# An fp32 encoder trunk on one core: order of work at the start, on the way into each MLP and at its end

## The chip, the core and the metric

The kernel runs on one core of one Trainium2 chip. The metric is the device time of one execution in microseconds (us), of which several runs are taken; beside them one execution is profiled. The engines are named as in the profile: PE (TensorE, matmuls; PEld its weight loads), DVE (VectorE), ACT (ScalarE), POOL (GpSimd) and SP (SyncE, which here only issues transfers). Each engine works through its own queue in order.

## The reference

A trunk of two layers over 256 tokens of width 2048, all in fp32. Layer 0 mixes tokens by 2-D neighbourhood attention, layer 1 by grouped-query attention with rotary positions; in both, four more heads attend to 256 memory tokens. Each layer ends with a squared-ReLU MLP of width 8192:

```python
m = rms_norm(mem, mem_norm)
h = x
for i in range(DEPTH):
    n = rms_norm(h, attn_norm[i])
    ...            # projection, attention heads -> mix
    km, vm = jnp.split(m @ w_mem_kv[i], 2, axis=-1)
    cross = memory_attention(qm, km, vm)
    h = h + jnp.concatenate([mix, cross], axis=-1) @ w_o[i]
    n = rms_norm(h, mlp_norm[i])
    h = h + jnp.square(jax.nn.relu(n @ w_up[i])) @ w_down[i]
return rms_norm(h, final_norm)
```

## The kernel before, in words

**Products.** Each fp32 operand is split into a high part (ACT, a copy to fp32r, line 299) and a low part (DVE, the difference, line 300), and a product is three matmuls: high by high, high by low, low by high. Weights come from HBM as chunks of 128 x 2048 (1 MB). A chunk is split and used in two halves, and one half is a *grain*: the unit in which the program is written. `run_all` walks over the grains; `ahead(n)` writes the loads, additions and splits of grains up to 8, 5 and 4 places further on before grain n is written (`SOON`), and `tick` releases work that `later(n, ...)` put off by n grains. What is written is not the final order: a planner builds each engine's queue from dependencies, priorities and a timing model of its own, and may pull forward whatever is ready. `keep_in_program_order` (`pin`) and `issue_after` are the ways to hold it.

**Buffers.** Raw up chunks have two buffers (tag `U`), their halves `uh` and `ul` two each, first parts of down chunks two (`b`), the tag `T` two (scaled activations `h_s`, then the down steps' `t`, then `raw_T`). PSUM has eight banks: four for attention and transposes (`ps_att`), four for accumulators (`ps_acc`); between MLP part 1 and the last part they are replaced by eight named sums (`ps_sums`: `up`, `p1` to `p7`).

**Start.** The memory's transposed features (`memT`) and the first two chunks of `w_km` come in quarters; `begin` splits and multiplies them quarter by quarter. The memory's squares (`mem_squares`), their sums (`mem_stats`) and the scaling of the first keys (`km_done`, `put`) are put off by ticks, so that other work goes first. `add_mem` asks for four key chunks, then four value chunks.

**Way into the MLP.** The output projection is done in four blocks of 512 columns (`o_done(layer, nb)`). After three blocks a provisional scale per token is known (`guard`); block b of `h` is then scaled on ACT (`scaled`, line 610), transposed on PE (line 317) and split into `hT` (lines 324, 325). The exact factor (`inv`) is applied at the end of the MLP. The fourth block is added to `h` (line 630), scaled, transposed and split in the same way, and `hT` is complete.

**MLP.** The hidden width is cut into 8 parts of 8 chunks. Part 0's up products (`up_grains`, lines 670 to 672) come alone; the first half of a chunk needs `hT` 0 to 7, the second 8 to 15. Then each step has one up chunk of the next part beside one down step (`down_grains`) of the part before. A down step forms products of 2 x 2 blocks with seven instead of eight multiplications: its preparation `pre` adds two blocks (line 758, DVE) and lets POOL add two others by an accumulating transfer (line 759), `prep_first` splits `b` into `bh`, `bl`, and `prep_second` adds twice more (lines 767, 768) and splits `t` into `th`, `tl`. The last part is done in the classical way (`plain_grains`): per block of 512 columns two chunks, the first split in halves (`uh`, `ul`), the second in one piece of 2048 (`th`, `tl`, one buffer). In the last block of layer 1 the products of the first 128 tokens are all issued before those of the others, and `finish` scales and stores.

Of the kernel before, what the change touches and what calls it, by code (L numbers as in the profile page):

```python
# [17 lines left out]
P = 128  # L18
# [52 lines left out]
def encoder_kernel(ctx: ExitStack, tc: tile.TileContext, t: dict, out: bass.AP):  # L71
# [23 lines left out]
    def open_sums():  # L95
        at.att = opened("ps_att", space=bass.MemoryType.PSUM, bufs=4)
        at.acc = opened("ps_acc", space=bass.MemoryType.PSUM, bufs=4)
# [31 lines left out]
    nc.scalar.activation(warm, mhalf[:, :1], AF.Exp)  # L129

# [166 lines left out]
    def split(dst_hi, dst_lo, src):  # L297

        nc.scalar.activation(dst_hi, src, AF.Copy)  # L299
        nc.vector.tensor_tensor(dst_lo, src, dst_hi.bitcast(F32), op=ALU.subtract)  # L300
# [10 lines left out]
    def transposed(dst, src, ks, which):  # L311

        for a in range(0, len(ks), 2):
# [4 lines left out]
            for b, k in enumerate(ks[a : a + 2]):  # L318
                split_pair(dst, pt[:, b, :], which, k)

    def split_pair(dst, src, which, k):

        g = gain(which, k)
        nc.scalar.activation(dst[:, k, :SEQ], src, AF.Copy, scale=g)
        nc.vector.scalar_tensor_tensor(dst[:, k, SEQ:], src, g, dst[:, k, :SEQ].bitcast(F32),  # L325
                                       op0=ALU.mult, op1=ALU.subtract)
# [115 lines left out]
    def km_done(layer, hd):  # L442
        def f(w):
            if layer == 0:
                later((5, 5, 1, 1)[hd], put, w)
# [35 lines left out]
    def add_mem(layer):  # L481
        for hd in range(NMH):
            add_s(t[f"w_km{layer}"][hd], get("memT"), km_done(layer, hd))
        add_m([t[f"w_vm{layer}"][c] for c in range(4)], parts_of("memT"), vm_done(layer))

# [110 lines left out]

    def o_done(layer, nb):
        which = 2 * layer

        def guard():  # L600
# [4 lines left out]
            box["hT"] = wide(f"hT{layer}")  # L605

# [17 lines left out]
        def f(w):  # L624
# [3 lines left out]
            for i in range(NT):  # L628
                hs = h[:, i, nb * 512 : (nb + 1) * 512]
                nc.vector.tensor_tensor(hs, w.ps[i], hs, op=ALU.add)  # L630
                if nb < 3:
                    sum_squares(which, i, nb)
            if nb == GUARD - 1:
                later(1, guard)
                for b in range(GUARD):
                    later(2 + 2 * b, scaled, b)
            if nb == 3:
                later(1, scaled, 3)
                for i in range(NT):
                    sum_squares(which, i, nb)  # L640
                later(2, inv)
# [32 lines left out]
    def half_of_side(raw, hf):  # L674
        tiles = tuple(at.side.tile([P, HALF], F32R, tag=n, bufs=2, name=n) for n in ("uh", "ul"))
        split(*tiles, raw[:, hf * HALF : (hf + 1) * HALF])
# [7 lines left out]
    def up_grains(layer, part, m):  # L684
# [8 lines left out]
        def run(hf):  # L693
            if hf == 0:
                if part == 0:
                    own["ps"] = at.acc.tile([P, 512], F32, tag="acc", name="ps_u")[:, :SEQ]
                else:
                    if part == 1 and m == 0:
                        closed("ps_acc", "ps_att")
# [40 lines left out]
    def down_grains(layer, part, n, begins, ends):  # L740
# [10 lines left out]

        def block(k):
# [42 lines left out]
        return [Grain(lambda: run("first", FIRST), lambda: after(FIRST), load, pre, prep_first, SOON),  # L795
# [403 lines left out]
```

## Time and profile before

| | |
|---|---|
| median of 3 runs | 2070.88 us (2068.25 to 2073.3) |
| the profiled execution's own time | 2069.22 us |
| its span, first to last instruction | 2067.2 us |
| mean granted clock of PE | 0.997 |
| busy: PE, DVE, ACT, POOL | 2039.7, 1668.6, 1251.3, 119.2 us |
| matmuls | 12516 |
| read from HBM | 398.17 MB |

Durations come from one profiled execution. A row of the timeline gives start, duration, engine, line, operation, output and inputs, and in brackets the idle time of the engine before it and what ended that. Matmul ends are modelled: one record of 256 columns lasts 0.28 us, while the next starts about 0.11 later, so how many matmuls a stretch holds tells more than how long PE was busy in it. The clock granted to PE is 1.00 or about 0.5.

### The profile page before, as it was taken

To read this page: it belongs to the slowest core of one execution; us is meant where nothing else is said; L and a number is where in the kernel's file an instruction comes from. 1 tells how busy PE (TensorE), PEld (TensorE's weight loads), DVE (VectorE), ACT (ScalarE), POOL (GpSimd) and SP (SyncE) were. 2 spreads that over 40 slices of the span, in tenths; PEclk is the share of its full clock that TensorE was granted. 3 is DMA by queue.
4 is the path that set the end of the run, shared out by engine and by line. 5 is a ranking of instruction groups with operands and counts; after the bars stand their busy time and mean duration, and the time that the engine had idled before them with its cause. 6 is when DMAs were issued, how large, how long until landed. Compare 5 with 4: busy or idle time off the path is not lost.

```text
span 2067.2 us, 31544 instructions
## 1 busy us (share of the span) xinstructions
PE 2039.7 (99%) x12516; PEld 1815.0 (88%) x12516; DVE 1668.6 (81%) x2047; ACT 1251.3 (61%) x1642; POOL 119.2 (6%) x144
## 2 busy tenths in 40 slices
PE   8999999999999999999999999999999999999998
PEld 6888888889999999999988888889999999999996
DVE  6767667566899999999996667666988999999896
ACT  6755555555666666666656557555666666666653
POOL 0000000000010000010000001000000000000000
PEclk9999999999999999999999999999999999999999
DMA  7755555736777787787765454536877787777773
GB/s 266 297 183 177 189 175 170 274 105 202 223 235 231 218 240 225 225 240 226 231 201 209 171 177 143 188 138 197 232 227 227 224 242 222 233 232 223 232 225 121
DMA packets 92996, 433.78 MB, mean 210 GB/s; under 512 B 10416, under 2 KB 12080, under 8 KB 59568
## 3 DMA queue, kind: packets, MB, share of 16 engines
q1 hardware_dynamic: 75456, 399.25, 57.3%
q0 software_dynamic: 16816, 31.46, 8.6%
q8 instruction: 98, 1.61, 0.3%
q10 hardware_dynamic: 576, 1.05, 0.1%
q14 instruction: 50, 0.41, 0.1%
HBM read 398.17 MB, written 4.19 MB: 195 GB/s over the span
## 4 chain that ended last, share of the span: by engine, by line
PE 97%; DVE 1%; issue 1%; DMA 1%; ACT 0%; SPq 0%; POOLq 0%; POOL 0%; DVEq 0%; ACTq 0%
PE ps_u L672 11%; PE ps_u L670 11%; PE ps_u L671 11%; PE p L779 9%; PE p L780 9%; PE p L781 9%; PE ps_m L205 8%; PE ps_m L208 8%; PE ps_m L209 8%; PE ps_s L218 7%; PE ps_s L221 3%; PE pt_a L379 1%; PE pt_n L317 0%; PE av L387 0%; PE sc_ps L353 0%
## 5 line engine op out<-in xcount | busy, mean ns | idle before, releaser
L671 PE MATMUL ps_u<-hT,uh 128*128 128x256 f32 x2048 | 569.3, 278 | 3.7 <-DVE hT L325 3.6
L670 PE MATMUL ps_u<-hT,uh 128*128 128x256 f32 x2048 | 569.9, 278 | 1.5 <-ACT uh L299 1.5
L672 PE MATMUL ps_u<-hT,ul 128*128 128x256 f32 x2048 | 569.3, 278 | 1.5 <-DVE ul L300 1.3
L299 ACT ACTIVATE uh<-raw_U 128x1024 fp32r<-128x1024 f32 x278 | 295.0, 1062 | 325.2 <-PE ps_u L671 301.9
L300 DVE TENSOR_TENSOR lo<-raw,hi 128x1024 fp32r<-128x1024 f32 (+1 forms) x222 | 266.3, 1204 | 167.7 <-ACT hi L299 166.4
L671 PEld LDWEIGHTS ps_u<-hT,uh 128*128 128x128 f32 x2048 | 385.9, 188 | 9.1 <-DVE hT L325 4.5
L670 PEld LDWEIGHTS ps_u<-hT,uh 128*128 128x128 f32 x2048 | 386.3, 189 | 7.6 <-ACT uh L299 1.9
L672 PEld LDWEIGHTS ps_u<-hT,ul 128*128 128x128 f32 x2048 | 387.1, 189 | 3.0 <-DVE ul L300 2.3
L300 DVE TENSOR_TENSOR ul<-raw_U,uh 128x1024 fp32r<-128x1024 f32 x278 | 337.9, 1219 | 35.4 <-ACT uh L299 35.4
L299 ACT ACTIVATE hi<-raw 128x1024 fp32r<-128x1024 f32 (+1 forms) x222 | 231.3, 1047 | 218.7 <-PE ps_m L209 116.1
L299 ACT ACTIVATE th<-t 128x2048 fp32r<-128x2048 f32 x112 | 215.2, 1921 | 124.9 <-PE p L781 118.2
L300 DVE TENSOR_TENSOR tl<-t,th 128x2048 fp32r<-128x2048 f32 x112 | 256.3, 2288 | 40.3 <-ACT th L299 39.9
L300 DVE TENSOR_TENSOR bl<-b,bh 128x1536 fp32r<-128x1536 f32 x112 | 196.1, 1751 | 0.4
L780 PE MATMUL p<-tl,a_s 128*128 128x512 f32 x448 | 177.2, 396 | 0.0
L781 PE MATMUL p<-th,a_s 128*128 128x512 f32 x448 | 174.4, 389 | 0.0
L299 ACT ACTIVATE bh<-b 128x1536 fp32r<-128x1536 f32 x112 | 166.2, 1484 | 6.4
L779 PE MATMUL p<-th,a_s 128*128 128x512 f32 x448 | 166.1, 395 | 0.0
L759 POOL DMA_DIRECT2D t<-b x112 | 97.0, 866 | 1168.3 <-DVE t L758 377.5
L218 PE MATMUL ps_s<-nT,hi 128*128 128x512 f32 x448 | 141.7, 394 | 0.0
L781 PE MATMUL p<-bh,a_s 128*128 128x512 f32 x336 | 131.1, 390 | 0.0
L780 PE MATMUL p<-bl,a_s 128*128 128x512 f32 x336 | 130.9, 390 | 0.0
L758 DVE TENSOR_TENSOR t<-t,b 128x512 f32<-128x512 f32 x112 | 77.2, 690 | 48.2 <-DMA t<-in_w_pair 36.4
(235 smaller groups left out, 3510.6 us busy)
## 6 DMA issues: line engine op xcount, KB each, us to landing
raw_U<-in_w_up SPq DMA_DIRECT2D x128, 1024.0 KB, 6.6
b<-in_w_pair SPq DMA_DIRECT2D x112, 768.0 KB, 4.5
raw<-in_w_o SPq DMA_DIRECT2D x32, 1024.0 KB, 5.0
t<-in_w_pair SPq DMA_DIRECT2D x112, 256.0 KB, 3.4
t<-b POOLq DMA_DIRECT2D x112, 256.0 KB, 6.6
raw<-in_w_b SPq DMA_DIRECT2D x21, 1024.0 KB, 5.0
raw<-in_w_av SPq DMA_DIRECT2D x12, 1024.0 KB, 4.9
raw<-in_w_aq SPq DMA_DIRECT2D x12, 1024.0 KB, 4.9
```

The lines of the kernel that those rows point to most:

```text
L205: first = nc.tensor.matmul(w.ps[i], ah, hi[:, s], start=st, stop=False)
L208: nc.tensor.matmul(w.ps[i], ah, lo[:, s], start=False, stop=False)
L209: nc.tensor.matmul(w.ps[i], al, hi[:, s], start=False, stop=sp)
L218: nc.tensor.matmul(ps, hi[:, s], acts[:, k0 + j, :], start=k0 + j == 0, stop=False)
L299: nc.scalar.activation(dst_hi, src, AF.Copy)
L300: nc.vector.tensor_tensor(dst_lo, src, dst_hi.bitcast(F32), op=ALU.subtract)
L670: nc.tensor.matmul(ps, hi[:, s], acts[:, k, :SEQ], start=k == 0, stop=False)
L671: nc.tensor.matmul(ps, hi[:, s], acts[:, k, SEQ:], start=False, stop=False)
L672: nc.tensor.matmul(ps, lo[:, s], acts[:, k, :SEQ], start=False, stop=k == KT - 1)
L779: nc.tensor.matmul(ps, a[:, 0, ai, :], hi[:, s], start=begins, stop=False)
L780: nc.tensor.matmul(ps, a[:, 0, ai, :], lo[:, s], start=False, stop=False)
L781: nc.tensor.matmul(ps, a[:, 1, ai, :], hi[:, s], start=False, stop=ends)
```

## The change

Seven things are done at once.

- The accumulator banks are opened before the attention banks, so that the two groups change places, also against the eight named sums of the MLP.
- Eleven matmuls of ones by ones are issued at the start, into a tile that nobody reads.
- The memory's squares and their sums are put off by one tick more and the first two keys' `put` by two more; the value chunks are asked for between the second and the third key chunk.
- In `o_done` the fourth block is no longer added and then scaled: `begun` scales the old `h` early, two scalar_tensor_tensor add the scaled sum from PSUM, and the transposes follow at once. The residual add, the squares and `inv` come 4, 6 and 8 grains later, behind the last of `hT` on ACT and DVE (`past`).
- Additions and splits of the first two down steps are queued on ACT and DVE behind the up split that was fourth from last when they are written (`behind`).
- Part 0's up chunks go two by two: both first halves, then both second halves.
- In the classical part the second chunk is split in halves too, into separate tiles (`bh`, `bl` and `th`, `tl`), and has two grains.

```diff
@@ -93,8 +93,8 @@
         pass
 
     def open_sums():
+        at.acc = opened("ps_acc", space=bass.MemoryType.PSUM, bufs=4)
         at.att = opened("ps_att", space=bass.MemoryType.PSUM, bufs=4)
-        at.acc = opened("ps_acc", space=bass.MemoryType.PSUM, bufs=4)
 
     def open_ring():
         at.ring = opened("ring")
@@ -128,6 +128,10 @@
     warm = const.tile([P, 1], F32, name="warm")
     nc.scalar.activation(warm, mhalf[:, :1], AF.Exp)
 
+    idle = at.att.tile([P, P], F32, tag="att", name="idle")
+    for _ in range(11):
+        nc.tensor.matmul(idle, ones, ones, start=True, stop=True)
+
     def gain(which, k):
         return gains[:, which * KT + k : which * KT + k + 1]
 
@@ -296,8 +300,8 @@
 
     def split(dst_hi, dst_lo, src):
 
-        nc.scalar.activation(dst_hi, src, AF.Copy)
-        nc.vector.tensor_tensor(dst_lo, src, dst_hi.bitcast(F32), op=ALU.subtract)
+        first = nc.scalar.activation(dst_hi, src, AF.Copy)
+        return first, nc.vector.tensor_tensor(dst_lo, src, dst_hi.bitcast(F32), op=ALU.subtract)
 
     def rstd_of(ss, n, name):
 
@@ -316,13 +320,14 @@
                 for i in range(NT):
                     nc.tensor.transpose(pt[:, b, i * P : (i + 1) * P], src(i, k), ident)
             for b, k in enumerate(ks[a : a + 2]):
-                split_pair(dst, pt[:, b, :], which, k)
+                last = split_pair(dst, pt[:, b, :], which, k)
+        return last
 
     def split_pair(dst, src, which, k):
 
         g = gain(which, k)
-        nc.scalar.activation(dst[:, k, :SEQ], src, AF.Copy, scale=g)
-        nc.vector.scalar_tensor_tensor(dst[:, k, SEQ:], src, g, dst[:, k, :SEQ].bitcast(F32),
+        first = nc.scalar.activation(dst[:, k, :SEQ], src, AF.Copy, scale=g)
+        return first, nc.vector.scalar_tensor_tensor(dst[:, k, SEQ:], src, g, dst[:, k, :SEQ].bitcast(F32),
                                        op0=ALU.mult, op1=ALU.subtract)
 
     def along_free(r, res):
@@ -442,7 +447,7 @@
     def km_done(layer, hd):
         def f(w):
             if layer == 0:
-                later((5, 5, 1, 1)[hd], put, w)
+                later((7, 7, 1, 1)[hd], put, w)
             else:
                 put(w)
 
@@ -479,9 +484,13 @@
             nc.gpsimd.dma_start(box["vm"][:, :, i, :], mem_v[:, i])
 
     def add_mem(layer):
-        for hd in range(NMH):
-            add_s(t[f"w_km{layer}"][hd], get("memT"), km_done(layer, hd))
+        def add_km(hds):
+            for hd in hds:
+                add_s(t[f"w_km{layer}"][hd], get("memT"), km_done(layer, hd))
+
+        add_km((0, 1))
         add_m([t[f"w_vm{layer}"][c] for c in range(4)], parts_of("memT"), vm_done(layer))
+        add_km((2, 3))
 
     mem_sq = at.work.tile([P, 512], F32, tag="b_o", bufs=3, name="mem_sq")
 
@@ -594,6 +603,12 @@
         nc.vector.tensor_scalar(v, s, 1.0 / (n * 512), EPS, op0=ALU.mult, op1=ALU.add)
         return v
 
+    def past(fn, ins=None):
+
+        a, v = ins or box["ready"]
+        with tc.issue_after(a.ins), tc.issue_after(v.ins):
+            fn()
+
     def o_done(layer, nb):
         which = 2 * layer
 
@@ -603,6 +618,13 @@
             box["scale"] = keep.tile([P, NT], F32, tag="scale", name="scale")
             nc.gpsimd.tensor_tensor(box["scale"], box["near"], mhalf[:, :NT], op=ALU.pow)
             box["hT"] = wide(f"hT{layer}")
+
+        def begun():
+
+            y = at.side.tile([P, NT, 512], F32, tag="T", bufs=2, name="h_s")
+            for i in range(NT):
+                nc.scalar.activation(y[:, i, :], h[:, i, D - 512 :], AF.Copy, scale=box["scale"][:, i : i + 1])
+            box["begun"] = y
 
         def scaled(b):
             y = at.side.tile([P, NT, 512], F32, tag="T", bufs=2, name="h_s")
@@ -625,20 +647,33 @@
             if nb == 0:
                 closed("work")
                 at.side = opened("side", side="right")
-            for i in range(NT):
-                hs = h[:, i, nb * 512 : (nb + 1) * 512]
-                nc.vector.tensor_tensor(hs, w.ps[i], hs, op=ALU.add)
-                if nb < 3:
+            def add():
+                for i in range(NT):
+                    hs = h[:, i, nb * 512 : (nb + 1) * 512]
+                    nc.vector.tensor_tensor(hs, w.ps[i], hs, op=ALU.add)
+
+            def squares():
+                for i in range(NT):
                     sum_squares(which, i, nb)
+
+            if nb < 3:
+                add()
+                squares()
             if nb == GUARD - 1:
                 later(1, guard)
                 for b in range(GUARD):
                     later(2 + 2 * b, scaled, b)
+                later(7, begun)
             if nb == 3:
-                later(1, scaled, 3)
+                y = box["begun"]
                 for i in range(NT):
-                    sum_squares(which, i, nb)
-                later(2, inv)
+                    nc.vector.scalar_tensor_tensor(y[:, i, :], w.ps[i], box["scale"][:, i : i + 1], y[:, i, :],
+                                                   op0=ALU.mult, op1=ALU.add)
+                box["ready"] = transposed(box["hT"], lambda i, k: y[:, i, k % 4 * P : (k % 4 + 1) * P],
+                                          list(range(12, KT)), (G_M0, G_M1)[layer])
+                later(4, past, add)
+                later(6, past, squares)
+                later(8, past, inv)
         return f
 
     def add_o(layer):
@@ -673,7 +708,7 @@
 
     def half_of_side(raw, hf):
         tiles = tuple(at.side.tile([P, HALF], F32R, tag=n, bufs=2, name=n) for n in ("uh", "ul"))
-        split(*tiles, raw[:, hf * HALF : (hf + 1) * HALF])
+        box.setdefault("splits", []).append(split(*tiles, raw[:, hf * HALF : (hf + 1) * HALF]))
         return tiles
 
     def loaded(src, tag):
@@ -696,7 +731,7 @@
                     own["ps"] = at.acc.tile([P, 512], F32, tag="acc", name="ps_u")[:, :SEQ]
                 else:
                     if part == 1 and m == 0:
-                        closed("ps_acc", "ps_att")
+                        closed("ps_att", "ps_acc")
                         at.sums = opened("ps_sums", space=bass.MemoryType.PSUM)
                         box["ps"] = {}
                     own["ps"] = at.sums.tile([P, 512], F32, tag="up", name="ps_u")[:, :SEQ]
@@ -749,6 +784,10 @@
             own["t"] = at.side.tile([P, 4, 512], F32, tag="T", bufs=2, name="t")
             nc.sync.dma_start(own["t"][:, 0, :], src[:, 3 * 512 :])
 
+        def behind(fn):
+
+            return (lambda: past(fn, box["splits"][-4])) if part == 0 and n < 2 else fn
+
         def block(k):
 
             return own["b"][:, k * 512 : (k + 1) * 512]
@@ -792,8 +831,8 @@
             if ends and (part, n) in FOLDS:
                 folded(q)
 
-        return [Grain(lambda: run("first", FIRST), lambda: after(FIRST), load, pre, prep_first, SOON),
-                Grain(lambda: run("second", SECOND), after_second, None, None, prep_second, SOON)]
+        return [Grain(lambda: run("first", FIRST), lambda: after(FIRST), load, behind(pre), behind(prep_first), SOON),
+                Grain(lambda: run("second", SECOND), after_second, None, None, behind(prep_second), SOON)]
 
     def columns_of(i, q, b):
         return h[:, i, q * 1024 + b * 512 : q * 1024 + (b + 1) * 512]
@@ -844,10 +883,10 @@
             if c == 0:
                 own[c, hf] = half_of_side(own[0], hf)
             else:
-                own[c, hf] = tuple(at.mlp.tile([P, CH], F32R, tag=x, name=x) for x in ("th", "tl"))
-                split(*own[c, hf], own[1])
-
-        PIECES = ((0, 0, 0, 2), (0, 1, 2, 2), (1, 0, 4, 4))
+                own[c, hf] = tuple(at.mlp.tile([P, HALF], F32R, tag="bt"[hf] + x, name=f"{x}_p") for x in "hl")
+                split(*own[c, hf], own[1][:, hf * HALF : (hf + 1) * HALF])
+
+        PIECES = ((0, 0, 0, 2), (0, 1, 2, 2), (1, 0, 4, 2), (1, 1, 6, 2))
 
         def begin():
             if nb == 0:
@@ -862,7 +901,7 @@
             if n == 0:
                 begin()
             for i in range(NT):
-                m_products(w, k0, nk, i, *own[c, hf], n == 0, n == 2)
+                m_products(w, k0, nk, i, *own[c, hf], n == 0, n == 3)
 
         def after():
             if not last:
@@ -872,12 +911,13 @@
             begin()
             for i in range(NT):
                 for n, (c, hf, k0, nk) in enumerate(PIECES):
-                    m_products(w, k0, nk, i, *own[c, hf], n == 0, n == 2, keep_order=True)
+                    m_products(w, k0, nk, i, *own[c, hf], n == 0, n == 3, keep_order=True)
                 w.done(w, i)
 
         return [Grain(lambda: run(0), None, lambda: load(0), None, lambda: prep(0, 0), SOON),
                 Grain(lambda: run(1), None, None, None, lambda: prep(0, 1), SOON),
-                Grain(lambda: run(2), after, lambda: load(1), None, lambda: prep(1, 0), SOON)]
+                Grain(lambda: run(2), None, lambda: load(1), None, lambda: prep(1, 0), SOON),
+                Grain(lambda: run(3), after, None, None, lambda: prep(1, 1), SOON)]
 
     SOON = (8, 5, 4)
     STEPS_OF = [(p, n) for p in range(PARTS - 1) for n in range(2 * STEPS)]
@@ -885,8 +925,9 @@
     FOLDS = {STEPS_OF[max(i for i, x in enumerate(HALF_OF) if x == q)] for q in range(2)}
 
     def add_mlp(layer):
-        for m in range(PK):
-            plan.extend(up_grains(layer, 0, m))
+        for m in range(0, PK, 2):
+            up = up_grains(layer, 0, m), up_grains(layer, 0, m + 1)
+            plan.extend(up[e][hf] for hf in range(2) for e in range(2))
         for x, (p, n) in enumerate(STEPS_OF):
             begins = x == 0 or HALF_OF[x - 1] != HALF_OF[x]
             ends = x == len(STEPS_OF) - 1 or HALF_OF[x + 1] != HALF_OF[x]
@@ -1068,9 +1109,9 @@
 
 
     for j in range(8):
-        later(1 + j // 2, mem_squares, j)
+        later(2 + j // 2, mem_squares, j)
     later(2, lambda: pin(nc.sync.dma_start(ident, t["ident"])))
-    later(5, mem_stats)
+    later(6, mem_stats)
     later(21, x_load)
     for j in range(8):
         later(24 + j, x_norm, j)
```

## The prediction, made before the changed kernel was run

> **What bounds the kernel now.** I read the page first, then the waits of PE, then windows around each wait.
>
> ```profile
> span 2067.2 us, 31544 instructions
> PE 2039.7 (99%) x12516; PEld 1815.0 (88%) x12516; DVE 1668.6 (81%) x2047; ACT 1251.3 (61%) x1642; POOL 119.2 (6%) x144
> ...
> PE ps_s L218 <- ACT hi L299: 8.5, 2, 7.0
> PE ps_u L671 <- DVE hT L325: 3.6, 2, 2.1
> ```
>
> PE has work for 99% of the span. The change takes no product away, so it can only win back holes in PE and stretches at half clock. The two longest waits lie at the two places the change names: the start (ACT's `hi` split) and the way into the MLP (DVE's `hT`). "Busy" hides part of a hole, since one matmul's record is longer than the step to the next, so I count matmuls per window. Columns: window, length, PE busy (x count), PEld, DVE, ACT, POOL, granted clock, DMA share, GB/s.
>
> ```profile
> 7.00:12.00 5.00, 4.97 (x16) 4.21 (x17) 4.76 (x10) 4.58 (x11) 0.00 (x0) 1.00 1.02 368
> 12.00:20.50 8.50, 8.50 (x50) 7.34 (x49) 6.65 (x15) 6.26 (x15) 0.00 (x0) 1.00 1.03 390
> 20.50:24.50 4.00, 2.06 (x10) 1.43 (x10) 3.25 (x5) 3.92 (x8) 0.00 (x0) 1.00 0.83 339
> 449.90:458.80 8.90, 5.84 (x40) 4.62 (x39) 7.28 (x14) 5.06 (x7) 0.88 (x1) 1.00 0.62 176
> 458.80:462.30 3.50, 3.50 (x17) 3.50 (x17) 3.19 (x5) 1.01 (x3) 0.87 (x1) 0.51 0.76 239
> 462.30:475.00 12.70, 12.70 (x114) 12.70 (x113) 7.52 (x11) 7.51 (x11) 0.00 (x0) 1.00 0.63 204
> 1388.40:1397.50 9.10, 5.78 (x39) 4.57 (x37) 6.92 (x12) 4.62 (x7) 0.90 (x1) 1.00 0.61 146
> 1397.50:1401.00 3.50, 3.19 (x15) 3.19 (x16) 3.10 (x7) 1.34 (x3) 0.86 (x1) 0.51 0.87 280
> 1401.00:1415.00 14.00, 14.00 (x125) 14.00 (x125) 9.02 (x12) 8.21 (x12) 0.00 (x0) 1.00 0.61 194
> ```
>
> An undisturbed up product takes 12.70/114 = 0.111 us in layer 0 and 14.00/125 = 0.112 in layer 1. So 449.90:458.80 lost 8.90 - 40 x 0.111 = 4.44 us, and the half clock behind it (0.51) lost 3.50 - 17 x 0.111 = 1.61. Layer 1 lost 9.10 - 39 x 0.112 = 4.73 and 3.50 - 15 x 0.112 = 1.82. The way in costs 12.60 us in all. At the start a product pair's mean step is 8.50/50 = 0.170: 7.00:12.00 lost 5.00 - 16 x 0.170 = 2.28, 20.50:24.50 lost 4.00 - 10 x 0.170 = 2.30.
>
> What holds the way in is DVE's order (start, duration, what; in brackets the idle time before and who ended it), with one row of ACT ahead:
>
> ```profile
> 447.60 0.71 ACT L610 ACTIVATE h_s<-h,scale 128x512 f32<-128x512 f32 x1
> 447.12 1.76 DVE L300 TENSOR_TENSOR bl<-b,bh 128x1536 fp32r<-128x1536 f32 x1
> ...
> 450.67 0.87 DVE L325 SCALAR_TENSOR_TENSOR hT<-pt_n,gains,hT 128x256 fp32r<-128x256 f32 x2
> ...
> 453.23 0.69 DVE L758 TENSOR_TENSOR t<-t,b 128x512 f32<-128x512 f32 x1 [1.62 <-DMA t<-in_w_pair]
> 453.84 2.29 DVE L300 TENSOR_TENSOR tl<-t,th 128x2048 fp32r<-128x2048 f32 x1
> 456.11 0.48 DVE L325 SCALAR_TENSOR_TENSOR hT<-pt_n,gains,hT 128x256 fp32r<-128x256 f32 x1
> ...
> 457.11 0.48 DVE L325 SCALAR_TENSOR_TENSOR hT<-pt_n,gains,hT 128x256 fp32r<-128x256 f32 x1
> 457.50 1.22 DVE L300 TENSOR_TENSOR ul<-raw_U,uh 128x1024 fp32r<-128x1024 f32 x1
> ```
>
> The first down steps' preparation (`bl`, `t`, `tl`), not needed until 16 up grains later, sits in front of the last two pieces of `hT` and of `ul`. Its `t` waits for a load, and everything behind it on DVE waits too.
>
> **The change, part by part.**
>
> *Way into the MLP.* The last block of columns now goes straight from the bank through two scalar_tensor_tensor (h times scale, `begun`, was made earlier) to the transposes; the two ACT copies at L610 (0.71 each; the second ended at 448.31) leave the path. Residual add, squares and `inv` follow later, behind `hT` on ACT and DVE. `behind` puts the two first steps' adds and splits after an up split four back. In front of `hT` then stand two DVE operations, eight transposes (under 8 x 0.111 = 0.9) and two pairs of ACT and DVE pieces (0.87 a pair): about 4 us, my estimate from these rows. As cover PE has the first halves of two chunks, 48 x 0.111 = 5.3 us, where it had 2.7; with only 2.7 some 1.3 would show. What the deferred add holds is two accumulator banks, first wanted by the third chunk four grains (10.7 us) on. The begun tile takes a T buffer, and SP's `t` loads queue behind it, but these steps now lie 16 grains away. POOL's accumulating DMAs follow the add at L758 and move later with it; nothing else is queued there. The swap of banks lets part 1's first up sum wait for one relu of part 0: 0 to 0.4 per layer, taken at 0, because a chunk's sum is usually an older one. I take 12.0 of the 12.60, ends 0 and 12.60.
>
> *Chunks two by two.* This part has a price. A raw chunk is freed when its second half is split. With two raw buffers its load has this much room:
>
> ```profile
> 458.75 39.65 SPq L681 DMA_DIRECT2D raw_U<-in_w_up  x8
> ...
> 469.61 1.23 DVE L300 TENSOR_TENSOR ul<-raw_U,uh 128x1024 fp32r<-128x1024 f32 x1 [0.38 <-ACT uh L299]
> ...
> L681 SPq DMA_DIRECT2D raw_U<-in_w_up x1: 328/328/328, 470.9 to 470.9; - x1
> ...
> DMA to landing us min/median/max: 4.8/4.8/4.8
> ...
> 476.68 1.06 ACT L299 ACTIVATE uh<-raw_U 128x1024 fp32r<-128x1024 f32 x1 [0.94 <-DVE c L733]
> 479.40 1.06 ACT L299 ACTIVATE uh<-raw_U 128x1024 fp32r<-128x1024 f32 x1 [0.82 <-PE ps_u L671]
> ```
>
> `ul` ended at 470.84, the load was issued at once, landed 4.8 later at 475.7, and was split from 476.68: 1.0 to spare. The product itself starts with the next slot, at 479.4, when PE frees its half tile; `uh` is ready at 477.74, 1.7 ahead, and `ul` 1.2 later, 0.5 ahead. So the margins are 2.7 for the high part and 1.5 for the low one. In the new order halves of two chunks alternate and a buffer is freed one slot, 2.72, later. High parts come just in time, low parts 1.2 late. There are four such places a layer (third, fifth and seventh chunk, each with its partner, then part 1's first). The cost is 0 to 8 x 1.2 = 9.6 us; PE can run the next high products first, so I take 0.5 each: 4.0.
>
> *First steps' preparation later.* Per step DVE has three adds (0.69), `bl` 1.76 and `tl` 2.29: 6.1 us. Two steps, 12.2 us a layer, move from the way in into these windows:
>
> ```profile
> 475.00:500.00 25.00, 25.00 (x216) 24.69 (x215) 15.68 (x23) 14.77 (x23) 0.00 (x0) 1.00 0.52 175
> 500.00:525.00 25.00, 25.00 (x171) 22.92 (x170) 20.37 (x20) 16.45 (x17) 0.87 (x1) 1.00 0.70 220
> 525.00:550.00 25.00, 25.00 (x162) 22.59 (x161) 22.11 (x26) 18.04 (x21) 2.61 (x3) 1.00 0.74 217
> 455.40:458.80 3.40, 1.50 (x9) 1.09 (x9) 3.40 (x8) 0.74 (x1) 0.06 (x1) 1.00 0.72 152
> ```
>
> DVE has 15.68 + 20.37 = 36.05 of 50 us there; with 12.2 it has 48.3, 97%, while the steady down stretch runs at 88% without a hole in PE. It fits in sum, but a 2.29 `tl` can stand before an `ul` that has 0.5 to spare. Cost 0 to 1.8 at each of four steps; I take 0.25 each: 1.0.
>
> *Head.* ACT and the third load:
>
> ```profile
> 17.31 0.62 ACT L494 ACTIVATE mem_y<-h 128x512 f32<-128x512 f32 x1
> 20.17 0.85 ACT L340 ACTIVATE km_a<-ps_s 128x256 f32<-128x256 f32 x2 [2.24 <-PE ps_s L221]
> 20.92 1.05 ACT L299 ACTIVATE hi<-raw 128x1024 fp32r<-128x1024 f32 x1
> ...
> L154 SPq DMA_DIRECT2D raw<-in_w_km x1: 328/328/328, 11.2 to 11.2; - x1
> ...
> DMA to landing us min/median/max: 7.2/7.2/7.2
> ```
>
> ACT idled 2.24 us for `km_a`, with the third chunk's `hi` behind it. `put` two ticks later and the squares one tick later take both away. Next in line is the load, landed at 11.2 + 7.2 = 18.4: `hi` can end at 19.5 instead of 21.97. The eleven idle matmuls run while PE waits for its first data (7.0 us); even at twice the 0.206 (3.50/17) of the half-clock row they take 4.5 us and cost nothing. They should warm the clock, but behind the cold products the next memory parts and splits come at their own pace. The order of `vm` and `km` changes no amount of work. Of 4.58 I take 2.0; ends 0 and 4.6.
>
> *Banks and the classical last part.*
>
> ```profile
> 1074.04 0.48 PE L205 MATMUL ps_m<-uh,a_p 128*128 128x512 f32 x1 [0.24 <-DVE z L813]
> 1076.40 0.50 PE L205 MATMUL ps_m<-uh,a_p 128*128 128x512 f32 x1 [0.72 <-DVE h L802]
> 2050.35 0.50 PE L208 MATMUL ps_m<-tl,a_p 128*128 128x512 f32 x1 [1.33 <-DVE tl L300]
> ```
>
> The first plain sums sat in the banks of `p5` and `p7`, emptied last; now they get those of `up` and `p3`, emptied a grain or more before: 0.24 + 0.72 = 1.0 us in layer 0. At the end PE waits 1.33 for one 2048-wide `tl`; two half splits into separate tiles let the first start one grain earlier: 1.3. The extra fixed cost of four half splits lies on ACT and DVE beside PE.
>
> Sum: 12.0 + 2.0 + 1.0 + 1.3 - 4.0 - 1.0 = 11.3 us won. The profiled execution took 2069.22, 1.7 below the median of the three runs, 2070.88 (2068.25 to 2073.3): 2057.9 on its scale, 2059.6 as a median. With every hole closed and no cost it is 19.5, 2051.4.
>
> [...] In 455.40:458.80 PE was busy 1.50 of 3.40, its longest wait there at most 2.1, and the clock was halved right after. [...]
>
> **The rivals.**
>
> *The pairs starve PE* (0.16). Low parts late at all eight places and no high products to fill in: 9.6 instead of 4.0 and both late steps at 0.5 more each (2.0): 3.7 us won, 2067.2. For it speaks the 1.5 of margin against 2.72; against it that the loads are only busy half the time, as the DMA share of 0.52 to 0.63 shows.
>
> *The order is not kept* (0.24). Instructions are queued by a planner, not as written; both halves of the first chunk may be split before the second chunk lands, since DMA brings it later. Then chunks run one by one as before: no pair cost, about 1 us lost at each way in. 12.0 - 2.0 + 4.3 - 1.0 = 13.3, 2057.6.
>
> *The blockage moves* (slower, 0.16). `tl` needs the `t` that POOL accumulates by DMA. If the planner puts that `tl` before an up split at both late steps of each layer, four places each cost what the way in costs now without the clock, about 4.6: 18.4. Then 16.3 - 4.0 - 18.4 = -6.1, 2077.0; with the half clock (1.7 a place), 2083.8. It decides from four such places on, or three with the clock. For it: DVE at 97%. Against: each has 16 grains, not a few, to prepare.
>
> [...]
>
> **How the numbers follow.** Forecast as summed 0.42. Faster by over 0.2% (4.1 us, about what a measurement of this kernel tells from none): 0.42 + 0.24 + 0.02 and a quarter of the starving case, 0.72. Within 0.2%: the rest of that case, 0.12. Slower: 0.16. The range goes from 2052.0 to 2073.0: all the holes closed at the one end, beyond the starving case with part of the blockage at the other; some 0.13 of the slower case lies above.
>
> **What would show it.** After the last output projection the DVE timeline has two scalar_tensor_tensor, four `hT`, then `ul`, and no `t`, `bl` or `tl`; no window there is at half clock. Raw_U loads of the first chunks come in pairs, and any wait of PE between 455 and 495 is for `uh` or `ul`. The first chunk after the start begins near 19.5. The waits on `z` at 1074 and on `tl` at 2050 are gone. The prediction is wrong if PE waits for `ul` by more than 1 us a pair, or if `tl` waits appear around the first down steps.

## The result and the profile after

The changed kernel takes 2074.4 us (median of 20 runs, 2070.83 to 2079.09) against 2070.58 for the kernel before (20 runs, 2067.74 to 2074.22). The ratio is 1.0019, 95% interval 1.0013 to 1.0026: 0.19% slower, where 11.3 us of gain were forecast. The profiled execution took 2076.84, 2.4 above the median.

From the page after, and from the list of PE's waits (us in total, times, longest):

```profile
span 2075.1 us, 31601 instructions
PE 2048.6 (99%) x12538; PEld 1821.9 (88%) x12538; DVE 1669.4 (80%) x2059; ACT 1252.5 (60%) x1650; POOL 120.1 (6%) x144
...
PE ps_u L707 <- DVE ul L304: 6.1, 8, 0.8
PE ps_u L705 <- ACT uh L303: 5.8, 6, 1.1
PE ps_m L209 <- ACT hi L303: 1.4, 1, 1.4
```

The wait for `hT` that stood second before is gone. In its place stand 14 short waits, 11.9 us, all in up products and all for a split of a raw up chunk. No one of them is over 1.1 us, so none of them stands out in a list by length; they show in the totals.

DVE on the new way in (the rows behind are left out):

```profile
444.13 0.75 DVE L670 SCALAR_TENSOR_TENSOR h_s<-ps_m,scale,h_s 128x512 f32<-128x512 f32 x1 [1.03 <-PE ps_m L213]
445.43 0.75 DVE L670 SCALAR_TENSOR_TENSOR h_s<-ps_m,scale,h_s 128x512 f32<-128x512 f32 x1 [0.54 <-PE ps_m L213]
449.41 1.23 DVE L304 TENSOR_TENSOR ul<-raw_U,uh 128x1024 fp32r<-128x1024 f32 x1 [3.23 <-ACT uh L303]
450.55 0.87 DVE L330 SCALAR_TENSOR_TENSOR hT<-pt_n,gains,hT 128x256 fp32r<-128x256 f32 x2
451.57 0.88 DVE L330 SCALAR_TENSOR_TENSOR hT<-pt_n,gains,hT 128x256 fp32r<-128x256 f32 x2 [0.15 <-ACT hT L329]
...
```

`bl`, `t` and `tl` are gone from here, as forecast. One thing is not as forecast: an `ul` of the third up split was put in front of the four `hT`.

The windows that answer to those before (window, length, PE busy (x count), PEld, DVE, ACT, POOL, granted clock, DMA share, GB/s):

```profile
7.00:12.00 5.00, 4.94 (x24) 3.64 (x24) 4.62 (x10) 4.55 (x10) 0.00 (x0) 1.00 1.01 359
12.00:19.30 7.30, 7.30 (x42) 6.24 (x41) 6.10 (x14) 5.46 (x13) 0.00 (x0) 1.00 1.02 370
19.30:23.30 4.00, 2.06 (x9) 1.26 (x8) 3.15 (x5) 3.91 (x8) 0.00 (x0) 0.97 1.01 418
23.10:26.50 3.40, 3.40 (x9) 2.62 (x9) 3.30 (x5) 3.40 (x6) 0.00 (x0) 0.50 0.78 248
449.40:454.40 5.00, 5.00 (x47) 5.00 (x46) 4.84 (x8) 3.84 (x9) 0.00 (x0) 1.00 0.70 223
454.40:460.00 5.60, 3.75 (x29) 3.14 (x28) 2.50 (x9) 2.45 (x6) 0.00 (x0) 1.00 0.63 221
460.00:463.40 3.40, 3.40 (x16) 3.40 (x17) 1.60 (x5) 1.90 (x2) 0.00 (x0) 0.50 0.02 7
```

At the start more products fit into 7.00:12.00, 24 instead of 16. The clock column has 1.00 for both, but the clock's first record is at 11.7 in the trace before and at 6.0 in the trace after, and nothing is recorded ahead of it. By their starts the first four products come 0.47 us apart before (7.03 to 8.91); as changed, behind the eleven idle matmuls (0.98 to 6.04), they come 0.32 apart (6.98 to 8.25). From 12.05 on it is 0.23 in the trace before. The hole one stage later is as large as before (2.06 busy of 4.00), and a stretch at half clock (0.50 in 23.10:26.50) follows it that was not there. On the way in, 449.40:454.40 holds 47 products, near the undisturbed 5.00/0.111 = 45: the old blockage is gone. Right behind it 5.60 us hold only 29, and the clock halves again (0.50 in 460.00:463.40). In that stretch the DMA share was 0.63, as in an undisturbed one before, and in a later starved one, 471.60:477.90, it was 0.30 with 34 products where 6.30/0.113 = 56 would fit: PE was short of chunks while the transfer engines had time to spare. (The 0.02 in 460.00:463.40 is no such case, since PE had work there and ran at half clock.)

The next columns of the same kind, 50 us from the first up product on: before, after, and of three experiments below (one by one, pairs alone, half loads).

```profile
444.80:494.80 50.00, 46.94 (x386) 45.72 (x385) 35.81 (x52) 30.12 (x44) 2.80 (x3) 0.97 0.56 174
```
```profile
445.20:495.20 50.00, 44.85 (x356) 42.81 (x355) 29.23 (x44) 25.87 (x38) 1.05 (x1) 0.97 0.41 137
```
```profile
444.20:494.20 50.00, 49.24 (x407) 47.97 (x406) 34.78 (x50) 31.19 (x46) 1.93 (x2) 1.00 0.53 168
```
```profile
445.80:495.80 50.00, 42.20 (x320) 40.22 (x319) 31.78 (x47) 26.32 (x39) 2.80 (x3) 0.93 0.52 169
```
```profile
444.70:494.70 50.00, 47.87 (x410) 47.26 (x409) 35.73 (x51) 30.67 (x45) 1.93 (x2) 0.99 0.63 188
```

The changed kernel does 30 products fewer than the kernel before in the stretch that it should have made denser; with the chunks one by one again it does 51 more than as changed.

### The profile page after: what moved, and what is told of

Its sections match the earlier page's. It is cut to its first block, busy times and chain, and to the rows that moved or that the text cites. A ratio compares the mean times of both kernels' runs of the same rounds, so it can differ in the third digit from the quotient of the medians.

```text
span 2075.1 us, 31601 instructions
## 1 busy us (share of the span) xinstructions
PE 2048.6 (99%) x12538; PEld 1821.9 (88%) x12538; DVE 1669.4 (80%) x2059; ACT 1252.5 (60%) x1650; POOL 120.1 (6%) x144
## 4 chain that ended last, share of the span: by engine, by line
PE 95%; DMA 2%; ACT 1%; DVE 1%; issue 0%; SPq 0%; POOLq 0%; POOL 0%; ACTq 0%
PE ps_u L707 11%; PE ps_u L705 11%; PE ps_u L706 10%; PE p L818 9%; PE p L819 9%; PE p L820 9%; PE ps_m L212 8%; PE ps_m L209 8%; PE ps_m L213 8%; PE ps_s L222 6%; PE ps_s L225 3%; DMA raw_U<-in_w_up 1%; DVE ul L304 1%; ACT uh L303 1%; PE pt_a L384 1%
## 5 line engine op out<-in xcount | busy, mean ns | idle before, releaser
L705 PEld LDWEIGHTS ps_u<-hT,uh 128*128 128x128 f32 x2048 | 386.3, 189 | 13.3 <-ACT uh L303 8.0
L304 DVE TENSOR_TENSOR ul<-raw_U,uh 128x1024 fp32r<-128x1024 f32 x278 | 337.4, 1218 | 47.3 <-ACT uh L303 43.5
```

What stands on the lines that cost most here:

```text
L304: return first, nc.vector.tensor_tensor(dst_lo, src, dst_hi.bitcast(F32), op=ALU.subtract)
L705: nc.tensor.matmul(ps, hi[:, s], acts[:, k, :SEQ], start=k == 0, stop=False)
```

## The experiments

Two theories stood at the start. **P**: the order in pairs frees each raw buffer a slot later, the loads come late, PE starves. **D**: the loss comes from another part of the change than the pairs. Each experiment ran beside the kernel before, in three sessions on two chips; "ratio" is always to the kernel before of the same session, and gains in us are worked out from it.

**Chunks one by one again** (`one_by_one`).

```
-        for m in range(0, PK, 2):
-            up = up_grains(layer, 0, m), up_grains(layer, 0, m + 1)
-            plan.extend(up[e][hf] for hf in range(2) for e in range(2))
+        for m in range(PK):
+            plan.extend(up_grains(layer, 0, m))
```

> The changed kernel with one edit: part 0's up chunks one by one again, as before the change. Theory P (the pairs starve PE: a raw chunk is held one slot of 2.72 us longer, its load comes late): the waits for uh and ul from 457 to 500 go in both layers, some 8 us a layer; some 1.5 to 3 us a layer show at the way in instead, since only 2.7 us of product cover the last hT. About 2058 to 2063 us, 0.994 to 0.996 of before. Rival D (the loss comes from the first down steps prepared late and the deferred add on DVE): pairs do not matter, 2070 to 2075.

Measured: 2059.86, ratio 0.9942 (0.9929 to 0.9954). This is P's figure. From 1.0019 to 0.9942 is 0.0077, some 15.9 us (13 to 19 by the two intervals): that is what the pairs cost. Of the waits for `ul` this is left:

```profile
PE ps_u L707 <- DVE ul L304: 1.8, 3, 0.8
```

**The pairs alone** (`pairs_alone`): the same three lines in the kernel before, nothing else.

> The kernel before with the chunk order two by two and nothing else. P: the late loads cost 5 to 8 us a layer, the old blockage on DVE is at most partly covered; 2073 to 2080 us, 1.001 to 1.005 of before. D: more products as cover, no new loss; 2066 to 2071.

Measured: 2087.76, ratio 1.0077 (1.0065 to 1.009): 16.0 us lost (13.5 to 18.6). That is above the 2080 of P's upper end, though its 5 to 8 us a layer would come to 16 at most; D's 2066 to 2071 is out. The pairs' price is the same with and without the rest of the change.

**Half loads** (`half_raws`): pairs as changed, but each raw up chunk comes as two loads of 512 KB into two of four half buffers, of the same size in sum; a half is free when that half is split. The edit holds for all up chunks. Its main part:

```
+        if tag == "U":
+            raws = []
+            for hf in range(2):
+                raws.append(at.side.tile([P, HALF], F32, tag=tag, bufs=4, name="raw_U"))
+                nc.sync.dma_start(raws[hf], src[:, hf * HALF : (hf + 1) * HALF])
+            return raws
```

> The changed kernel, pairs kept, but each raw up chunk is loaded as two halves of 512 KB into four half buffers (same memory), each freed by its own split. P: the loads are no longer late, 2057 to 2062 us, 0.993 to 0.996 of before. If what is late is not the buffer but the rate of loading: no gain, 2072 to 2077. D: 2071 to 2076.

Measured: 2059.67, ratio 0.9938 (0.9926 to 0.9951), as good as one by one. So it is not the order of the products that costs, but how long it holds the buffers. The raw loads of the three kernels in their steady stretch (count, duration of the issue, first and last start; then issue to landing, min/median/max), first the changed kernel, then one by one, then half loads:

```profile
L716 SPq DMA_DIRECT2D raw_U<-in_w_up x5: 327/327/328, 466.5 to 494.2; - x5
...
DMA to landing us min/median/max: 4.8/4.9/6.2
```
```profile
L716 SPq DMA_DIRECT2D raw_U<-in_w_up x5: 327/328/328, 460.1 to 482.2; - x5
...
DMA to landing us min/median/max: 4.8/5.0/6.3
```
```profile
L719 SPq DMA_DIRECT2D raw_U<-in_w_up x7: 327/328/328, 459.3 to 475.6; - x7
...
DMA to landing us min/median/max: 4.4/4.6/4.7
```

A chunk's 48 products need 48 x 0.113 = 5.4 us of PE (0.113 is the mean step of these products). One by one, five loads start within 22.1 us, 5.5 apart: PE sets the pace. Half loads start (475.6 - 459.3)/6 = 2.7 apart, 5.4 a chunk. In pairs they are (494.2 - 466.5)/4 = 6.9 apart: 1.5 us lost per chunk. The load itself takes about the same time in all three, 4.9, 5.0 and for a half 4.6 us; the 0.3 that a half lands sooner is small against the 2.6 found below. What the cycle consists of stands in the queues of ACT and DVE (and PE's two waits below them) for one pair:

```profile
471.45 1.06 ACT L303 ACTIVATE uh<-raw_U 128x1024 fp32r<-128x1024 f32 x1 [0.87 <-DMA raw_U<-in_w_up]
...
475.54 1.06 ACT L303 ACTIVATE uh<-raw_U 128x1024 fp32r<-128x1024 f32 x1 [2.24 <-DMA raw_U<-in_w_up]
476.51 0.94 ACT L303 ACTIVATE a_s<-c 128x896 fp32r<-128x896 f32 x1
477.35 1.04 ACT L303 ACTIVATE uh<-raw_U 128x1024 fp32r<-128x1024 f32 x1
480.62 1.06 ACT L303 ACTIVATE uh<-raw_U 128x1024 fp32r<-128x1024 f32 x1 [2.23 <-PE ps_u L706]
```
```profile
478.78 1.22 DVE L304 TENSOR_TENSOR ul<-raw_U,uh 128x1024 fp32r<-128x1024 f32 x1
```
```profile
473.82 0.38 PE L707 MATMUL ps_u<-hT,ul 128*128 128x256 f32 x1 [0.75 <-DVE ul L304]
477.92 0.39 PE L707 MATMUL ps_u<-hT,ul 128*128 128x256 f32 x1 [0.76 <-DVE ul L304]
```

The first chunk's buffer is asked for again at 466.5. Its first half is split at 471.45 as soon as it lands. There are two half tiles `uh`, and the other one goes to the second chunk's first half, whose load came 2.7 behind and lands at 475.5. So the first chunk's second half gets a tile only when the products of its first half end, at 476.6. It is split from 477.35 on, behind a split of activations (`a_s`), and its `ul` ends at 480.0. Then the next load starts: 13.5 us after the last, where two chunks give PE 10.9 us of work. With one chunk after the other the second half gets the other tile, a slot earlier.

**One pair only** (`pair_first`): the first two chunks of part 0 as a pair, the other six one by one.

> The changed kernel with only the first two chunks of part 0 as a pair and the other six one by one. Theory C (a cycle: with two raw buffers, each freed one slot later, a pair's loads and splits take 13.5 to 14.2 us from load to load where PE needs 10.9, so every pair costs again): what the first pair costs stays, in the changed kernel 1.17 + 0.92 at 457 to 459 and 1.6 at half clock, some 3.7 a layer over one_by_one, and the later pairs' 4 to 5 a layer go: 2066 (2063 to 2069). Rival W (all of it comes from the first pair, beside the way in, and is only handed on): 2072 to 2075. Rival O (the first pair is covered by chunks loaded ahead): 2060.

Measured: 2060.17, ratio 0.9941 (0.9927 to 0.9954). Both C's 2066 and W fall; O's number came. That the later pairs cost holds, since without them no loss against one_by_one is left (0.9941 and 0.9942). That the first pair costs 3.7 a layer does not: its chunks are loaded before the MLP begins, and the first load behind them starts at 450.9. The profiled execution, 2063.38 against the median's 2060.17, waits here:

```profile
PE ps_u L707 <- DVE ul L304: 2.1, 4, 0.8
PE ps_u L705 <- ACT uh L303: 2.0, 2, 1.6
```

So the first pair makes two waits for the third chunk's `uh`, 0.5 us in layer 0 and 1.6 in layer 1, and this execution's mean granted clock was 0.997, where its four others had 0.998 to 0.999; in the median nothing of it is left to see. How often it costs the clock stays open.

**Without `behind`** (`one_nobehind`): one_by_one, with the first down steps' preparation free to be queued as the planner likes.

> As one_by_one, and additions and splits of the first two down steps no longer held behind an up split. P: they come back in front of hT or ul at the way in, 2 to 5 us a layer slower than one_by_one, 2063 to 2071 us. D: same as or faster than one_by_one.

Measured: 2067.53, ratio 0.9981 (0.9972 to 0.999): 0.0039, 8 us, are lost against one_by_one. DVE on the way in:

```profile
447.78 1.75 DVE L304 TENSOR_TENSOR bl<-b,bh 128x1536 fp32r<-128x1536 f32 x1
451.39 2.29 DVE L304 TENSOR_TENSOR tl<-t,th 128x2048 fp32r<-128x2048 f32 x1 [1.86 <-ACT th L303]
453.60 1.22 DVE L304 TENSOR_TENSOR ul<-raw_U,uh 128x1024 fp32r<-128x1024 f32 x1
454.73 0.87 DVE L330 SCALAR_TENSOR_TENSOR hT<-pt_n,gains,hT 128x256 fp32r<-128x256 f32 x2
```

The blockage is back, 1.86 us of idle DVE included. So `begun` pays little without `behind`: with the banks and the end it makes the 4 us that are left. Whether `behind` pays without `begun` was not run.

**The way in alone** (`way_alone`): the kernel before with `begun`, the deferred residual work and `behind`; no pairs, old head, old banks, old last part.

> The kernel before with the new way into the MLP alone (begun tile, two STTs, deferred add, squares and inv, `behind`): no pairs, no idle matmuls, old head, old banks, old last part. Theory S (the parts add up, and what one_by_one gained between the first up product and the first plain product, 4.2 us in layer 0 and 3.3 in layer 1, is the way in alone): 7.4 us below the kernel before, about 2064 (2062 to 2066), with the end still waiting 1.33 for tl and the first plain sums still waiting for z. Rival F (the prediction's term, 12.0 of the 12.60 lost there): about 2060. Rival N (the way in pays only together with the other edits): within 2 us of the kernel before.

Measured: 2062.03, ratio 0.9956 (0.9944 to 0.9968), 9.1 us (6.6 to 11.6). The 7.4 lies inside the interval, the prediction's 12.0 just outside. But 12.0 was meant with pairs as cover; for chunks one by one the prediction took 1.0 a layer off it (its rival "The order is not kept"), and that 10.0 lies inside. The parts about add up: 9.1 here, and 12.0 (9.5 to 14.7) for everything but the pairs.

**The third up split behind `hT`** (`one_late_uh`): one_by_one with the split that stood in front of the last four `hT` queued behind them.

> one_by_one with the third up split (uh and ul) queued behind the last hT pieces on ACT and DVE, instead of in front of the last four. Theory U (that split is the last piece of the blockage on the way in: one_by_one still waits 0.92 for ul at 454 and 0.26 and 0.93 at 1387): hT is done about 1 us earlier, those waits go, 1 to 2 us won, 2058 to 2059. Rival V (the third split then becomes the late one: its ul ends near 453.5 and the products that need it could start at 452.9): no change or up to 1 us worse, 2059.9 to 2061.

Measured: 2060.18, ratio 0.9947 (0.9935 to 0.9958): no gain, as V said. Counted from the first up product, ACT began the last two `hT` 4.7 us on instead of 5.8, and PE then waited for that split instead:

```profile
452.31 0.39 PE L707 MATMUL ps_u<-hT,ul 128*128 128x256 f32 x1 [1.31 <-DVE ul L304]
```

Theory U also had the wrong split. A half chunk is 24 products, and by their count PE's wait in one_by_one is in the fourth half, not in the third. Its split stands on ACT behind the deferred squares (`sq`), which wait for the residual add. PE's row and, from ACT, the two rows in question (one between them left out):

```profile
455.01 0.39 PE L707 MATMUL ps_u<-hT,ul 128*128 128x256 f32 x1 [0.76 <-DVE ul L304]
```
```profile
452.03 0.63 ACT L595 ACTIVATE sq<-h 128x512 bf16<-128x512 f32 x1 [1.15 <-DVE h L653]
...
452.66 1.04 ACT L303 ACTIVATE uh<-raw_U 128x1024 fp32r<-128x1024 f32 x1
```

No run puts the squares behind that split.

**The old head** (`one_old_head`): one_by_one without idle matmuls, with the old ticks, and four key chunks first.

> one_by_one with the old head: no idle matmuls, put, squares and statistics at their old ticks, all four km chunks ahead of vm. Theory H0 (the head's edits gain nothing, because km_a still stands in front of the third chunk's hi): the same as one_by_one, 2059.9 within 1, first nT product near 101.3. Rival H2 (the prediction's term, 2.0 won in the head): 2061.9, first nT product near 103.

Measured: 2059.56, ratio 0.9944 (0.9931 to 0.9956): the same as one_by_one. The intervals alone would leave some 4 us either way, but the traces agree: the first product of layer 0's projection (the nT product) starts at 101.0 here, at 101.1 in one_by_one and at 101.3 in the kernel before. So the new head gains nothing that shows. What it was meant to do did not happen, by ACT in the changed kernel:

```profile
19.01 0.85 ACT L345 ACTIVATE km_a<-ps_s 128x256 f32<-128x256 f32 x2 [1.84 <-PE ps_s L225]
19.75 1.05 ACT L303 ACTIVATE hi<-raw 128x1024 fp32r<-128x1024 f32 x1
```

Two more ticks did not put `km_a` behind the third chunk's `hi`. ACT still idles 1.84 us for `km_a`, as it did 2.24 before, with `hi` behind it, whose load had landed at 18.6. `hi` itself starts 1.2 us earlier than before (20.92); why nothing of that is left at the projection, the runs don't show.

**`km_a` really behind** (`one_km_after`): the split that must come first is named, not a tick.

```
-                later((7, 7, 1, 1)[hd], put, w)
+                later((7, 7, 1, 1)[hd], *((lambda: past(lambda: put(w), box["ring"][0]),) if hd < 2 else (put, w)))
```

`box["ring"]` holds the splits of the chunks from the third on.

> one_by_one with the two first km evaluations really queued behind the third chunk's hi and lo on ACT and DVE. Theory K (km_a in front of hi makes PE's holes of 1.58 and 0.69 us near 20): hi starts when the load has landed, near 18.7 instead of 19.7, the holes shrink by 1.0 to 1.6 us in sum, first nT product near 99.8, total 2058.5 (2057.5 to 2059). Rival L (the next load or the squares are late anyway): the hole moves to the fourth chunk and the first nT product stays at 101.1, 2059.9.

Measured: 2058.22, ratio 0.9937 (0.9925 to 0.9949). In time that is 1 to 2 us less than one_by_one, which the intervals alone don't separate; the trace shows K's mechanism. ACT here, then the stretch around the hole in one_by_one (first window) and here (second):

```profile
18.86 1.06 ACT L303 ACTIVATE hi<-raw 128x1024 fp32r<-128x1024 f32 x1 [1.52 <-DMA raw<-in_w_vm]
```
```profile
19.50:23.50 4.00, 2.06 (x10) 1.23 (x9) 2.81 (x5) 3.87 (x7) 0.00 (x0) 1.00 0.99 414
```
```profile
19.50:23.50 4.00, 3.56 (x18) 2.70 (x17) 3.38 (x4) 4.00 (x9) 0.00 (x0) 1.00 1.01 422
```

Now the load releases `hi`, and PE is busy 3.56 of 4.00 instead of 2.06. In the four executions that have this edit (here and three below) the first nT product starts at 99.4 to 99.8, in the ten others at 100.8 to 102.7.

**The same edit in the kernel before** (`before_km`).

> The kernel before with one edit: the first two km evaluations queued behind the third chunk's split on ACT and DVE (there the third chunk is the third km chunk). Theory K: of the 2.30 us lost at 20.5 to 24.5 some 1.6 go, 1.6 below the kernel before, about 2069.0. Rival M (it pays only with vm as third chunk and warm products): no change.

Measured: 2070.55, ratio 0.9992 (0.9984 to 1.0001): 1.7 us by the ratio, but no change isn't excluded. In the trace the stage from the first product to the first nT product is 1.7 us shorter, 92.6 instead of 94.3; the same execution lost part of that again in layer 1, where the clock stayed halved for 6.8 us (0.50) instead of 3.4 (0.50 in 1397.51:1400.92 of the kernel before):

```profile
1393.90:1400.70 6.80, 6.46 (x28) 6.17 (x29) 5.08 (x8) 2.52 (x4) 0.86 (x1) 0.50 0.91 246
```

**Both cures** (`one_half_km`): one by one, half loads, `km_a` behind.

> one_by_one with both cures: raw up chunks loaded as halves in four half buffers, and the km evaluations queued behind the third chunk's split. Theory A (the two lie in different stages and add up): the head's 1.6 of one_km_after and, of the 0.46 and 1.24 that one_by_one waits at the end of the up chunks of layer 1, about 1: 2057 (2056 to 2058.5). Rival B (half loads are worth nothing once chunks run one by one, since a buffer has three slots of 2.7 us against a load of 5): as one_km_after, 2058.2.

Measured: 2057.61, ratio 0.993 (0.9917 to 0.9942), 14.5 us below the kernel before. A's figure, but one_km_after's 2058.22 is too near to say that the half loads add anything once chunks run one by one.

**More idle matmuls** (`best18`): the same with 18 instead of 11.

> one_half_km with 18 idle matmuls instead of 11. In one_km_after the idle matmuls ended at 5.0, the first data came at 7.13, and the clock was halved from 7.77 to 11.18; in one_by_one data came at 6.50 and it was not. Theory G (seven more, some 0.2 us each at full clock, close that hole): no half-clock window before 12 and 0 to 1.5 us less than one_half_km. Rival T (the head waits for the load of the third chunk anyway, landed near 18.6): the same as one_half_km within 0.5, whatever the clock does.

Measured: 2057.23, ratio 0.9929 (0.9917 to 0.9942), the best time of all, yet not to be told from the one before. The granted clock was 1.00 in 5.00:12.00 and in 12.00:19.40, and 0.999 in the mean of the execution:

```profile
5.00:12.00 7.00, 6.95 (x41) 6.07 (x41) 5.42 (x11) 5.55 (x12) 0.00 (x0) 1.00 0.97 342
```

The first nT product came at 99.8 nevertheless, at 99.4 in one_half_km, as rival T said. A full clock in front of a stage that waits for the third chunk bought nothing here.

## Why the prediction was wrong, point by point

- **The failing step is "Chunks two by two".** 4.0 us were taken, 9.6 was the bound; it cost 15.9. The mechanism was named rightly (a buffer freed a slot later, low parts late), and the size went wrong in three places. First, "PE can run the next high products first, so I take 0.5 each": PE kept its queue's order, in which every third product needs `ul`, and behind a half's first two products it stood still, about 0.76 each time. Second, four places a layer of 1.2 each were counted; the list has 14 waits in both layers, because each partner is late by itself, for `uh` or for `ul`, and none of the time is made up: the cycle of 13.5 against 10.9 is late anew in every pair. The 2.7 and 1.5 of margin were read as a reserve for one event, where a full cycle had to be added up: load, the first half's split and products, the second half's split. Third, the waits cost the clock, which the sum put at nothing for this part: in the profiled execution once a layer 3.4 us at half speed (0.50 granted in 459.98:463.39 and in 1402.06:1405.47), one product every 0.214 us, 16 instead of 30, 1.6 lost in each.
- **What the pairs cost in the trace.** The two profiled executions can be compared directly. From the first up product to the first down product the changed kernel takes 55.8 and 56.9 us, one_by_one 47.3 and 48.1: 17.3 more. Of this, 10.1 are listed waits (11.9 less the 1.8 that one_by_one keeps), 3.2 the clock, and some 1.8 the part of 11 more holes that the list doesn't count (0.16 each, an estimate: a record lasts 0.28 and the next normally starts 0.12 after it). The other 2.2 lie in holes too short for the list. The median holds less of it than this execution, 15.9.
- **The rival "The pairs starve PE"** (0.16) was the right one, and was priced by the same count: 3.7 won instead of 3.8 lost. Its "against", that the loads are only busy half the time, was no argument: in a starved stretch the DMA share was 0.30, because no buffer was free to load into.
- **"The order is not kept"** fell: loads came in pairs and the products followed. **"The blockage moves"** fell too: `tl` stands in front of an up split once a layer (499.4 and 1441.4, 2.3 us each), but PE never waits for `tl` or for the `ul` behind it, and that the median's 2074 lies near this rival's 2077 has another cause, the pairs. Late preparation, 1.0, can't be seen by itself: at the first down step of layer 1 one_by_one waits 1.1 us, but for `c`, the last up chunk's square, on ACT.
- **Way into the MLP**, 12.0 with pairs as cover, 10.0 without: 9.1 (6.6 to 11.6) without. The blockage and its half-clock stretch went as worked out: the granted clock was 0.97 in 444.80:494.80 of the kernel before and 1.00 in 445.40:495.40 of way_alone, whose mean is 0.999. What was overlooked is what is late next: with the third up split in front of `hT` PE waits 0.8 us for the fourth, with it behind `hT` 1.3 for the third.
- **Head**, 2.0: nothing. The step "`put` two ticks later and the squares one tick later take both away" took the tick for an order; as written `put` comes behind that `hi`, and the planner pulled `km_a` forward. The next step, the load near 18.4 and `hi` to end at 19.5, was about right: with `km_a` held back `hi` ends at 19.9.
- **Banks**, 1.0, and **end**, 1.3: right by the traces. Between the first plain product of layer 0 and the first output projection of layer 1 the changed kernel and one_by_one take 198.4 us, the kernel before and way_alone 199.6; from the first plain product of layer 1 to the last matmul it is 44.2 against 45.8. The waits on `z`, `h` and `tl` are gone.
- **The sum.** Without the price of the pairs the terms come to 15.3, and to 13.3 for chunks one by one, as the rival "The order is not kept" had it; 12.0 (9.5 to 14.7) came. The pairs then took 15.9. The range, 2052 to 2073, missed by 1.4; its upper end rested on part of the blockage coming back, not on a larger price of the pairs. The 0.02 among the chances stands for a case that no run shows: between the first product and the last the halved clock (0.50 to 0.51) came behind waits of PE of at most 2.1 us in the kernel before and 1.4 in the changed one.
- **The signs.** No `t`, `bl` or `tl` on the way in, loads in pairs, waits for `uh` or `ul` alone, no waits on `z` and `tl` at the end: all came. The sign of being wrong, more than 1 us a pair for `ul`, did not: 6.1 us over eight pairs is 0.8. It looked at `ul` alone, and the waits for `uh` are as long.

## What to carry to other kernels

When an edit reorders work over a ring of buffers, add up the whole cycle of one buffer (load, wait for a free tile and for the split's turn, split, free) and compare it with the engine's work per turn of the ring: a cycle that is longer by 2.6 of 10.9 us is paid at every turn, and a margin at one place says little. If the order is wanted, free the buffer in smaller pieces: the same bytes in halves removed all of the 15.9 us. And work put off by a count of steps isn't ordered: where a planner may pull it forward, name the instruction that must come first, and read each queue afterwards.

## What the hardware showed

In these traces the clock halved without one long wait. In 454.40:460.00 of the changed kernel PE was busy 3.75 of 5.60 us, its longest listed wait 1.0, and the next 3.4 us ran at 0.50. In the kernel before, the longest waits ahead of its two halvings (0.50 in 458.85:462.26 and in 1397.51:1400.92) were 1.54 and 2.10. Nor did the same hole always cost the clock: the one near 20 left 2.06 us busy of 4.00 both in the changed kernel (19.30:23.30) and in one_by_one (19.50:23.50), and behind it the first was granted 0.50 (23.10:26.50), the second 1.00 (23.50:27.00). What decides it, no run shows.

A load of half the size took nearly as long, 4.6 us (half_raws) instead of 4.9 to 5.0 for the whole chunk (changed kernel, one_by_one). Halves were asked for twice as often, every 2.7 us, and still came in time. In time such loads cost nothing that shows: 2059.67 us for half_raws, 2059.86 for one_by_one.
